# Block 2's latent attention: two heads together in the column halves of TensorE, and query tiles packed six for eight

## The chip, the core and the metric

The kernel runs on one core of one Trainium2 chip. Such a core has five engines, each with its own queue of instructions: TensorE (matrix products into the accumulator memory PSUM; called PE in the profile, and PEld for its weight loads), VectorE (DVE), ScalarE (ACT), GpSimd (POOL) and SyncE (SP, which here issues the weight transfers). The metric is the device time of one execution in microseconds (us); lower is better. All data are fp32. A dense product is made of three TensorE products of operands split into a high and a low part (line 416, `mm3`: 420, 421 and 422 are its three matmuls), in a one-pass type. A plain fp32 matmul shows in the profile as two MATMUL instructions, each of which takes a column of the moving operand in about twice the time.

## The reference

Two blocks of a model, each of two layers, on 256 tokens of width 1024; the second block has a second stream, a context of 256 tokens. What matters here is the attention in each mixing layer of the second block: eight heads, with queries and keys of 64 plain and 32 rotated features, and values of 64.

```python
def mla_q(q_lat, q_norm, w_uq, cos, sin):
    q = (rmsnorm_2(q_lat, q_norm) @ w_uq).reshape(b, n, MLA_HEADS, QK_NOPE + QK_ROPE)
    q_nope, q_rope = q[..., :QK_NOPE], q[..., QK_NOPE:]
    q_rope = apply_axial_rope(q_rope, cos, sin)
...
def attend(q_nope, q_rope, k_nope, k_rope, v):
    s = (jnp.einsum("bqhd,bkhd->bhqk", q_nope, k_nope)
         + jnp.einsum("bqhr,bkr->bhqk", q_rope, k_rope)).astype(jnp.float32) * ATTN_SCALE
    p = jax.nn.softmax(s, axis=-1).astype(v.dtype)
    return jnp.einsum("bhqk,bkhd->bqhd", p, v)
```

The latent `q_lat` has 384 features. In the first mixing layer (l = 0) the queries of the 256 tokens look at 512 keys (tokens and context), and the context's own 256 queries at the context's 256 keys. In the second (l = 1) only the tokens have queries, with 512 keys. In the diff and below, ns is the number of streams with queries, 2 and then 1.

## The kernel before

Weights come in one stream of units of at most 128 x 1024, in the order of a plan; SP loads them some units ahead, and ACT and DVE split each into its two parts (lines 393 and 394) up to three ahead of its use. The framework sets the order of instructions in each engine's queue before the run, by priority in the order of the program and by what it estimates to be ready; so a product may stand in the trace between two steps that follow each other in the code.

`mix` (line 1210) is one mixing layer. After the projections, the Fourier mixer and the convolution it makes the attention:

- Keys, K: four products, for two heads each, copied into a tile for each head of 128 rows with the rotated key rows beside the plain ones (lines 1266 to 1269).
- Queries: `queries` (line 1356) makes one 128-row tile for each head out of a weight that is padded with zeros: 3 tiles of the latent times 3 matmuls, nine for a head, over 512 columns in layer 0 and 256 in layer 1. ACT copies it out of PSUM (line 1368), and `rope2` (line 1346) rotates its 32 rows by a matmul over 256 columns (line 1349, two instructions) and three DVE operations (lines 1352 to 1354). It is a generator; `attend` calls its steps a pair of heads ahead, the first pair's lie before the values.
- Values, V: tokens on the partitions, four tiles (line 1280 copies them).
- `attend` (line 1391) goes through blocks of one head and 128 queries: in layer 0, for each of four pairs of heads, 4 blocks with 512 keys and then 4 with 256, 32 blocks in all; in layer 1, 16 blocks with 512 keys.

A block is, in this order: scores by one fp32 matmul (line 1375); softmax with queries on the partitions (`softmax_rows`: maximum on DVE, line 818; times minus the scale, 819; exponential on ACT, 479, with its sums read out behind it; reciprocal, 823, and product with it, 825, on DVE); and two blocks later (`AHEAD`) `values`: transposes of the weights on TensorE, one for 128 keys (line 1385), a copy of them by ACT into a tile `pt` (1387), and the product with the values, 128 queries by 64 features for 128 keys each (line 1389, two instructions a product, four products for 512 keys). This last one takes 64 of TensorE's 128 columns: those of the upper or the lower half, as its output rows do, by the head (a = 0 or 1). An accumulator `o` in PSUM takes a pair of heads and 256 queries, and ACT copies it out (line 1413).

PSUM has eight banks of 512 columns, handed out by name: three for `mm` (scores, dense products), three for `ax` (transposes, rotations, and `o`), one each for `nm` (sums of the norms) and `md`. Afterwards the output projection (`project_out`, key "mo") runs over all eight tiles of the mixers; its first products may start on the tiles that are there.

Of the kernel before, what the change touches and what calls it, by code (L numbers as in the profile page):

```python
# [16 lines left out]
T = 256  # L17
# [11 lines left out]

# ---------------------------------------------------------------- weight stream  # L30
# A unit is a [128, n] tile of weights, n <= 1024, made of blocks
# (array, leading index, first row, first column, width).

# [13 lines left out]
def _spread(units, mods, every):  # L47
    """The modulation units one by one between the others: the first three at once."""
    out, mods = mods[:3], mods[3:]
    for i, u in enumerate(units):  # L50
        out.append(u)
        if i % every == every - 1 and mods:
            out.append(mods.pop(0))
    return out + mods


def _evenly(units, mods, a, b, kind="acc"):
    """The modulation units evenly between the units a to b from the end."""
# [21 lines left out]
def _mix_units(l):  # L80
# [7 lines left out]
    for p in range(4):  # L88
        if p == 1:
            u.append(("mat", ("uv", l), [("w_ukv_v", l, kt * 128, 0, 512) for kt in range(2)]))  # L90
        u.append(("mat", ("uq", l, p), [("w_uqp", l, kt * 128, (2 * p + i) * 128, 128)
                                        for i in range(2) for kt in range(3)]))
# [52 lines left out]
def pack_weights(inp):  # L145
# [11 lines left out]
    qp = np.zeros((2, 384, 8, 128), np.float32)  # L157
    qp[:, :, 0::2, 0:96] = uq[:, :, 0::2]
    qp[:, :, 1::2, 0:32] = uq[:, :, 1::2, 64:]
    qp[:, :, 1::2, 64:128] = uq[:, :, 1::2, :64]  # L160
    arr["w_uqp"] = qp.reshape(2, 384, 1024)
# [11 lines left out]
# ---------------------------------------------------------------- small vectors and constants  # L173
# [48 lines left out]
def constants():  # L222
    """Masks, rotations, the DFT and the axial rotation tables: functions of the shapes alone."""
# [66 lines left out]
class Unit:  # L290
# [4 lines left out]
# Tiles of each phase: tag -> (columns, buffers)  # L295
# [16 lines left out]
class Builder:  # L312
# [26 lines left out]
    # ---- tiles  # L339
# [34 lines left out]
    # ---- weights  # L374
# [32 lines left out]
    def flush(self, n=len(PLAN)):  # L407
        """The modulation units that stand next in the stream, up to n."""
# [7 lines left out]
    def mm3(self, out, u, j, ah, al, start, stop, w=128):  # L416
        """out += W[:, block j]^T a"""
# [6 lines left out]
    def mmt(self, out, ah, al, u, j, start, stop, w=512):  # L424
        """out += a^T W[:, block j]"""
# [6 lines left out]
    def gemm(self, u, h, c0, c1, p=None):  # L432
        """One 128-feature tile of a product over the tiles of h, columns c0..c1."""
# [6 lines left out]
    def lead(self, units, h, c0, c1):  # L440
        """The same for some units at once, tile by tile of h as they come."""
# [7 lines left out]
    def pair(self, tag, n):  # L449
        """The two parts of an operand, in one tile or two."""  # L450
# [5 lines left out]
    def split(self, src, hi, lo):  # L456
        """hi + lo = src, each exact in one pass."""
# [4 lines left out]
    def table(self, name):  # L462
        """The scalar engine's table set from here on, in the order of the program."""
# [7 lines left out]
    def after(self, i, j):  # L471
        """Instruction i goes to its engine's queue behind j."""
# [3 lines left out]
    def act(self, out, src, func, **k):  # L476
        """A function of the scalar engine that needs a table."""
# [41 lines left out]
    def settle(self):  # L519
        """The sums over the partitions that are due."""  # L520
# [30 lines left out]
    def gain(self, name, l, gname, ch):  # L551
        """g * (1 + scale), per stream."""
# [56 lines left out]
    def enter(self, st, ns, A, B, lead):  # L609
        """h = x * r * A + B, split, stream by stream; lead starts on each stream as it is ready."""  # L610
# [9 lines left out]
    def enter_raw(self, st, A, B):  # L620
        """r, and for each tile of x the parts of x * A with those of B as more columns (an even number): of a product over
        them, the columns times r plus the last one are the product over x * r * A + B."""
# [27 lines left out]
    def project_out(self, units, src, ns, gate, st, tail=True):  # L650
        """x += gate * W^T src, tile by tile; the last tiles stream by stream, so that the norm of one
        stream runs beside the products of the other. With one stream, the first tiles at once, so that the
        last of src has time to arrive."""
# [16 lines left out]
    # ---- swiglu  # L670
    def ffn(self, key, st, ns, A, B, gate, more, before_last=None):
        """x += gate * swiglu(x * r * A + B); returns the sums of squares of the new x."""
# [53 lines left out]
    # ---- block 1, layer 0: softmax heads and stick-breaking heads  # L726
# [26 lines left out]
    def vproj(self, key, h):  # L753
        """Values with tokens on the partitions: two tiles [128, 512]."""
# [16 lines left out]
    def headsplit(self, src):  # L771
        """A tile of two heads' rows, each head in its own copy with zeros for the other."""
# [5 lines left out]
    def av(self, pt, v, hp):  # L778
        """Output rows of a pair of heads from their weights [k, (k0 q0, k0 q1, k1 q1)]."""
# [576 lines left out]
    def queries(self, l, p, ql, no):  # L1356
# [3 lines left out]
        for i in range(3):  # L1360
            if last is not None:
                self.rope2(last, slice(64, 96) if i == 1 else slice(0, 32))
# [229 lines left out]
```

## Time and profile before

| | |
|---|---|
| median of 3 runs | 2563.02 us (2561.24 to 2563.8) |
| span of the profiled execution, first to last instruction | 2561.5 us |
| TensorE (PE) busy in the span | 98% |
| VectorE (DVE) busy | 66% |
| ScalarE (ACT) busy | 44% |
| GpSimd (POOL) busy | 8% |
| mean granted TensorE clock | 0.996 of full |

The profile has one execution; no time of its own is given for that but its span, which lies 1.5 us under the median of the runs. Busy time on PE runs from the start of a matmul to its modelled end, so consecutive matmuls overlap and a busy PE isn't one at its peak: what a matmul costs in a stream is the distance from its start to the next start. The attention lies at 1339 to 1421 us (layer 0) and 2286 to 2337 us (layer 1) of the span.

### The profile page before, as it was taken

The numbers are of one execution on the slowest core, as the hardware profiler recorded it, in microseconds if no ns is written. First come the engines' busy times: TensorE is split into PE (matmuls) and PEld (weight loads), VectorE is DVE, ScalarE is ACT, GpSimd is POOL, SyncE is SP. The second block draws the span as 40 slices with busy tenths as digits, with TensorE's granted clock in tenths as the row PEclk, the third lists the DMA queues.
The fourth block names the chain that finished last, engine by engine and source line by source line (L and its number), as shares of the span: only waits on it lengthen the run. The fifth ranks groups of instructions, "written<-read, shape, count | busy, mean of one in ns | idle before, by whom it ended". The sixth has DMA issues, their size and how long they took to land.

```text
span 2561.5 us, 39957 instructions
## 1 busy us (share of the span) xinstructions
PE 2501.8 (98%) x15915; PEld 2177.1 (85%) x15915; DVE 1689.1 (66%) x2607; ACT 1128.5 (44%) x1955; POOL 195.9 (8%) x183
## 2 busy tenths in 40 slices
PE   6999999999999999999999999999999999999998
PEld 5878998988999887878886888888888888888998
DVE  6857768765887957774646474565656565675665
ACT  4556456565645523233525432323432323555544
POOL 1004100423000100001000100000100000101000
PEclk9999999999999999999999999999999999999999
DMA  8767656324875545663220243454244453232553
GB/s 333 268 209 244 212 188 208 116 83 158 286 248 181 189 160 188 187 197 124 79 79 26 70 154 110 146 175 144 91 159 162 150 178 122 92 109 83 190 183 97
DMA packets 117402, 408.38 MB, mean 159 GB/s; under 512 B 13024, under 2 KB 16352, under 8 KB 117216
## 3 DMA queue, kind: packets, MB, share of 16 engines
q1 hardware_dynamic: 114192, 403.08, 47.8%
q10 hardware_dynamic: 3024, 2.75, 0.4%
q8 instruction: 125, 2.05, 0.3%
q14 instruction: 61, 0.50, 0.1%
HBM read 404.74 MB, written 1.05 MB: 158 GB/s over the span
## 4 chain that ended last, share of the span: by engine, by line
PE 93%; DVE 3%; DMA 2%; ACT 1%; issue 1%; POOL 0%; ACTq 0%; DVEq 0%; SPq 0%
PE pmm L420 25%; PE pmm L422 25%; PE pmm L421 25%; PE pmd L516 2%; PE pax L1389 2%; PE pax L1072 2%; PE pmm L1375 1%; DMA r<-w 1%; PE pax L421 1%; PE pax L422 1%; PE pax L420 1%; PE pax L1385 1%; DVE l L394 1%; PE pnm L607 1%; PE pmm L429 0%
## 5 line engine op out<-in xcount | busy, mean ns | idle before, releaser
L393 ACT CAST h<-r 128x1024 fp32r<-128x1024 f32 (+3 forms) x545 | 550.2, 1016 | 1025.5 <-PE pmm L421 937.6
L394 DVE TENSOR_TENSOR l<-r,h 128x1024 fp32r<-128x1024 f32 (+3 forms) x545 | 658.6, 1213 | 306.0 <-ACT h L393 296.1
L420 PE MATMUL pmm<-h,h 128*128 128x512 f32 (+1 forms) x1928 | 674.3, 351 | 6.7 <-ACT h L640 2.3
L421 PE MATMUL pmm<-h,h 128*128 128x512 f32 (+1 forms) x1928 | 669.1, 348 | 2.0 <-DVE h L641 1.9
L422 PE MATMUL pmm<-h,l 128*128 128x512 f32 (+1 forms) x1928 | 668.9, 347 | 1.0 <-DVE l L394 1.0
L420 PEld LDWEIGHTS pmm<-h,h 128*128 128x128 f32 x1928 | 365.3, 190 | 64.4 <-issue 9.3
L421 PEld LDWEIGHTS pmm<-h,h 128*128 128x128 f32 x1928 | 365.5, 190 | 49.6 <-DVE h L641 3.2
L422 PEld LDWEIGHTS pmm<-h,l 128*128 128x128 f32 x1928 | 365.3, 190 | 47.6 <-DVE l L394 1.5
L420 PE MATMUL pmm<-hid,h 128*128 128x256 f32 (+1 forms) x1053 | 349.5, 332 | 0.0
L422 PE MATMUL pmm<-hid,l 128*128 128x256 f32 (+1 forms) x1053 | 347.5, 330 | 0.3 <-DVE l L394 0.3
L421 PE MATMUL pmm<-hid,h 128*128 128x256 f32 (+1 forms) x1053 | 347.4, 330 | 0.0
L510 DVE SCALAR_TENSOR_TENSOR macc<-r,cond,macc 128x1024 f32<-128x1024 f32 x266 | 330.0, 1281 | 0.3 <-DMA r<-w 0.2
L420 PE MATMUL pmm<-hb,h 128*128 128x258 f32 x1008 | 287.3, 285 | 7.0 <-DVE s L681 6.4
L422 PE MATMUL pmm<-hb,l 128*128 128x258 f32 x1008 | 285.8, 284 | 0.0
L421 PE MATMUL pmm<-hb,h 128*128 128x258 f32 x1008 | 285.3, 283 | 0.0
L420 PEld LDWEIGHTS pmm<-hid,h 128*128 128x128 f32 x1053 | 200.1, 190 | 20.3 <-ACT h L393 1.2
L422 PEld LDWEIGHTS pmm<-hid,l 128*128 128x128 f32 x1053 | 200.1, 190 | 18.7 <-DVE l L394 0.5
L421 PEld LDWEIGHTS pmm<-hid,h 128*128 128x128 f32 x1053 | 200.1, 190 | 18.2
L647 DVE SCALAR_TENSOR_TENSOR x<-pmm,mod_w_mod,x 128x256 f32<-128x256 f32 x188 | 84.6, 480 | 176.5 <-PE pmm L422 176.2
L420 PEld LDWEIGHTS pmm<-hb,h 128*128 128x128 f32 x1008 | 191.6, 190 | 9.8 <-DVE s L681 7.2
L422 PEld LDWEIGHTS pmm<-hb,l 128*128 128x128 f32 x1008 | 192.4, 191 | 0.4 <-issue 0.4
L421 PEld LDWEIGHTS pmm<-hb,h 128*128 128x128 f32 x1008 | 192.4, 191 | 0.3 <-DVE hb L630 0.2
(337 smaller groups left out, 2891.7 us busy)
## 6 DMA issues: line engine op xcount, KB each, us to landing
r<-w SPq DMA_DIRECT2D x665, 512.0 KB, 4.3
r<-w SPq DMA_DIRECT2D x96, 448.0 KB, 3.3
r<-w SPq DMA_DIRECT2D x16, 256.0 KB, 3.0
r<-w SPq DMA_DIRECT2D x8, 384.0 KB, 3.4
const<-const SPq DMA_DIRECT2D x2, 960.0 KB, 6.1
x<-xT ACTq DMA_DIRECT2D x8, 128.0 KB, 4.6
x<-ctxT ACTq DMA_DIRECT2D x8, 128.0 KB, 3.4
out<-x ACTq DMA_DIRECT2D x4, 128.0 KB, 2.1
```

Source lines behind the costliest of these rows:

```text
L393: nc.scalar.copy(h[:, :n], r[:, :n])
L394: nc.vector.tensor_tensor(lo[:, :n], r[:, :n], h[:, :n].bitcast(F32), op=OP.subtract)
L420: nc.tensor.matmul(out, wh, ah, start=start, stop=False)
L421: nc.tensor.matmul(out, wh, al, start=False, stop=False)
L422: nc.tensor.matmul(out, wl, ah, start=False, stop=stop)
L510: self.nc.vector.scalar_tensor_tensor(a, r, w, a, op0=OP.mult, op1=OP.add)
L516: self.nc.tensor.matmul(p[32 * g:32 * g + 32, :256], w, r[:, 256 * g:256 * g + 256], start=start, stop=stop)
L607: nc.tensor.matmul(p, self.ones, s[:, cg], start=tot == 1, stop=True)
L647: self.nc.vector.scalar_tensor_tensor(v, p[:, s * T - c0:s * T + T - c0], gate[:, 8 * s + m:8 * s + m + 1], v, op0=OP.mult, op1=OP.add)
L1072: nc.tensor.matmul(p[:, s], a[:, s], b[:, s], start=True, stop=True)
L1375: self.nc.tensor.matmul(s, q, k, start=True, stop=True)
L1389: nc.tensor.matmul(o, V[b], pt[:, 128 * b:128 * b + 128], start=b == 0, stop=b == nb - 1)
```

## The change

The attention goes through blocks of two heads. A block's scores and softmaxes are made for both heads; two blocks later both are transposed and copied (`turned`, which now stands ahead of the next block's scores in the program, while the product with the values stands behind them), and their products with the values are issued in turns, a product of the one head and one of the other. `o` moves from the three `ax` banks to the one `nm` bank. The query weight is packed without zeros: two tiles with the 32 rotated rows of four heads each, which are rotated whole, and four tiles with the 64 plain rows of two heads each. A head's tile is put together from both: ACT copies the plain half, DVE the rotated rows, and POOL sets 32 rows of the odd heads to zero. Even heads have 96 rows in queries and keys. There is one more `tmp` tile, and the plan has three units for the queries in place of four. Lines that are only blank or comments are left out, and so are the old bodies, which stand above.

```diff
-    for p in range(4):
-        if p == 1:
+    u.append(("mat", ("ur", l), [("w_uqr", l, kt * 128, r * 128, 128) for r in range(2) for kt in range(3)]))
+    for i in range(2):
+        u.append(("mat", ("un", l, i), [("w_uqn", l, kt * 128, (2 * i + j) * 128, 128)
+                                        for j in range(2) for kt in range(3)]))
+        if i == 0:
             u.append(("mat", ("uv", l), [("w_ukv_v", l, kt * 128, 0, 512) for kt in range(2)]))
-        u.append(("mat", ("uq", l, p), [("w_uqp", l, kt * 128, (2 * p + i) * 128, 128)
-                                        for i in range(2) for kt in range(3)]))
...
-    arr["w_uqp"] = qp.reshape(2, 384, 1024)
+    arr["w_uqn"] = uq[:, :, :, :64].reshape(2, 384, 512)
+    arr["w_uqr"] = uq[:, :, :, 64:].reshape(2, 384, 256)
...
-    "mix": {"h": (512, 18), "t": (256, 2), "raw": (512, 6), "tmp": (512, 4), "o": (512, 8), "pt": (512, 4), "ru": (256, 1)},
+    "mix": {"h": (512, 18), "t": (256, 2), "raw": (512, 6), "tmp": (512, 5), "o": (512, 8), "pt": (512, 4), "ru": (256, 1)},
...
-        self.rope2(kr, slice(0, 128))
+        self.rope2(kr)
...
-        queries = [self.queries(l, p, ql, no) for p in range(4)]
         u = self.get(("uk", l))
...
-                K += [a, b]
-        Q = list(queries[0])
+                K += [a[0:96], b]
+        qr = self.rotated(l, ql, no)
+        first = self.queries(l, 0, ql, qr, no)
         u = self.get(("uv", l))
...
-        self.attend(Q, queries, K, V, ns, out)
+        self.attend(lambda p: self.queries(l, p, ql, qr, no) if p else first, K, V, ns, out)
...
+        nc.vector.tensor_tensor(u, ps[:, :T], tab[:, T:], op=OP.mult)
+        nc.vector.tensor_tensor(t[:, :T], t[:, :T], tab[:, :T], op=OP.mult)
+        nc.vector.tensor_tensor(t[:, :T], t[:, :T], u, op=OP.add)
+
+    def latent(self, u, j, ql, no):
+        ps = self.mm()
+        for kt in range(3):
+            self.mm3(ps[:, :no], u, 3 * j + kt, ql[kt][0], ql[kt][1], kt == 0, kt == 2)
+        return ps[:, :no]
+
+    def rotated(self, l, ql, no):
+        u = self.get(("ur", l))
+        out = []
+        for r in range(2):
+            q = self.t("raw")
+            self.nc.scalar.copy(q[:, :no], self.latent(u, r, ql, no))
+            out.append(q)
+        for q in out:
+            self.rope2(q)
+        return out
+
+    def queries(self, l, p, ql, qr, no):
+        nc = self.nc
+        if p % 2 == 0:
+            self.un = self.get(("un", l, p // 2))
+        ps = self.latent(self.un, p % 2, ql, no)
+        a, b = self.t("raw"), self.t("raw")
+        r, j = qr[p // 2], 64 * (p % 2)
+        nc.gpsimd.memset(b[32:64, :no], 0.0)
+        nc.vector.tensor_copy(a[64:96, :no], r[j:j + 32, :no])
+        nc.vector.tensor_copy(b[0:32, :no], r[j + 32:j + 64, :no])
+        nc.scalar.copy(a[0:64, :no], ps[0:64])
+        nc.scalar.copy(b[64:128, :no], ps[64:128])
+        return a[0:96], b
...
+    def turned(self, P):
+        n = P.shape[-1]
+        p = self.ax()[:, :n]
+        for b in range(n // 128):
+            self.nc.tensor.transpose(p[:, 128 * b:128 * b + 128], P[:, 128 * b:128 * b + 128], self.ident)
+        pt = self.t("pt")[:, :n]
+        self.nc.scalar.copy(pt, p)
+        return pt
+
+    def attend(self, queries, K, V, ns, out):
+        nc = self.nc
+        Q = {0: queries(0)}
+        blocks = [(p, s, qt) for p in range(4) for s in range(ns) for qt in range(2)]
+        P, o = {}, None
         for i in range(len(blocks) + AHEAD):
+            pts = [self.turned(w) for w in P.pop(i - AHEAD)] if i >= AHEAD else None
             if i < len(blocks):
+                p, s, qt = blocks[i]
                 q0, k0 = s * T + 128 * qt, s * T
+                P[i] = [self.weights(Q[p][a][:, q0:q0 + 128], K[2 * p + a][:, k0:]) for a in range(2)]
+                if i % (2 * ns) == 2 * ns - 2 and p < 3:
+                    Q[p + 1] = queries(p + 1)
+            if pts:
+                p, s, qt = blocks[i - AHEAD]
+                if qt == 0:
+                    o = self.psum("nm", 1)
+                nb = 4 - 2 * s
+                for b in range(nb):
+                    for a in range(2):
+                        h = slice(128 * p + 64 * a, 128 * p + 64 * a + 64)
+                        nc.tensor.matmul(o[64 * a:64 * a + 64, 128 * qt:128 * qt + 128], V[2 * s + b][:, h],
+                                         pts[a][:, 128 * b:128 * b + 128], start=b == 0, stop=b == nb - 1)
+                if qt == 1:
+                    nc.scalar.copy(out[p][:, s * T:s * T + T], o[:, :T])
```

## Rows read from the trace of the kernel before

**Rows 1.** The profile's first part: busy us, share of the span, instructions of each engine.

```profile
PE 2501.8 (98%) x15915; PEld 2177.1 (85%) x15915; DVE 1689.1 (66%) x2607; ACT 1128.5 (44%) x1955; POOL 195.9 (8%) x183
```

**Rows 2.** The chain of work that ended last, shares of the span by engine.

```profile
PE 93%; DVE 3%; DMA 2%; ACT 1%; issue 1%; POOL 0%; ACTq 0%; DVEq 0%; SPq 0%
```

**Rows 3.** Busy time by stretch (start:end, length; busy us and instructions; clock).

```profile
1339.00:1421.00 82.00, 81.10 (x433) 54.02 (x432) 51.85 (x158) 47.85 (x122) 0.00 (x0) 1.00 0.08 27
2286.00:2304.00 18.00, 16.82 (x93) 11.39 (x92) 15.10 (x38) 10.95 (x25) 0.00 (x0) 1.00 0.17 58
...
2286.00:2337.00 51.00, 49.82 (x300) 34.81 (x300) 34.32 (x94) 29.35 (x70) 0.00 (x0) 1.00 0.13 42
```

**Rows 4.** Groups of instructions, 1339 to 1421 us: count, busy us, mean ns, idle before.

```profile
L1389 PE MATMUL pax<-pt,h 128*64 128x128 f32 x192 | 27.5, 281 | 0.9 <-ACT pt L1387 0.6
...
L825 DVE TENSOR_SCALAR tmp<-tmp,s 128x512 f32<-128x512 f32 x16 | 7.7, 484 | 0.2
L479 ACT ACTIVATE tmp<-pmm,s 128x256 f32<-128x256 f32 x16 | 7.6, 480 | 0.6 <-DVE s L819 0.6
L818 DVE TENSOR_REDUCE s<-pmm 128x1 f32<-128x256 f32 x16 | 6.6, 415 | 1.1 <-PE pmm L1375 1.0
...
L825 DVE TENSOR_SCALAR tmp<-tmp,s 128x256 f32<-128x256 f32 x16 | 5.6, 351 | 0.1
...
L1349 PE MATMUL pax<-raw,const 128*128 128x256 f32 x12 | 3.9, 405 | 0.0
...
L1353 DVE TENSOR_TENSOR raw<-raw,const 32x256 f32<-32x256 f32 x6 | 2.4, 405 | 0.0
```

**Rows 5.** The same for 2286 to 2337 us.

```profile
L1389 PE MATMUL pax<-pt,h 128*64 128x128 f32 x128 | 16.8, 279 | 0.0
```

**Rows 6.** Timeline at two places where two value products follow each other (start, length).

```profile
1409.10 1.89 PE L1389 MATMUL pax<-pt,h 128*64 128x128 f32 x16
...
1409.26 0.58 ACT L1387 COPY pt<-pax 128x512 f32<-128x512 f32 x1 [0.28 <-PE pax L1385]
...
1410.92 0.48 PE L1375 MATMUL pmm<-h,raw 128*128 128x256 f32 x1
...
2332.51 1.58 PE L1389 MATMUL pax<-pt,h 128*64 128x128 f32 x16
```

**Rows 7.** Timeline: one modulation product in four column quarters.

```profile
78.34 0.64 PE L516 MATMUL pmd<-macc,pick 128*32 128x256 f32 x8
```

**Rows 8.** Timeline: dense matmuls over 512 and 256 columns, and a rotation.

```profile
1330.98 0.39 PE L422 MATMUL pmm<-h,l 128*128 128x512 f32 x1
1331.21 0.39 PE L420 MATMUL pmm<-h,h 128*128 128x512 f32 x1
1331.44 0.63 PE L1349 MATMUL pax<-raw,const 128*128 128x256 f32 x2
...
2285.46 0.28 PE L422 MATMUL pmm<-h,l 128*128 128x256 f32 x1
2285.58 0.28 PE L420 MATMUL pmm<-h,h 128*128 128x256 f32 x1
```

**Rows 9.** Waits, first two of 1339 to 1421 us, then two of 2286 to 2337 us.

```profile
PEld pax L1389 <- ACT pt L1387: 13.1, 27, 0.8
DVE s L823 <- ACT tmp L479: 13.1, 17, 1.4
...
PEld pax L1389 <- ACT pt L1387: 2.8, 6, 0.8
PEld pax L1389 <- ACT o L1413: 0.8, 1, 0.8
```

**Rows 10.** Timeline of one head's softmax in layer 1.

```profile
2330.10 0.69 DVE L818 TENSOR_REDUCE s<-pmm 128x1 f32<-128x512 f32 x1 [2.47 <-PE pmm L1375]
...
2331.07 0.69 ACT L479 ACTIVATE tmp<-pmm,s 128x512 f32<-128x512 f32 x1 [0.69 <-DVE s L819]
...
2332.08 0.48 DVE L825 TENSOR_SCALAR tmp<-tmp,s 128x512 f32<-128x512 f32 x1
```

More of the change, by code (lines that the diff above doesn't have):

```diff
@@ L156, in pack_weights @@
     uq = inp["w_uq_2"].reshape(2, 384, 8, 96)
[L157 to L160, printed above, removed]
-    arr["w_uqp"] = qp.reshape(2, 384, 1024)
+    arr["w_uqn"] = uq[:, :, :, :64].reshape(2, 384, 512)
+    arr["w_uqr"] = uq[:, :, :, 64:].reshape(2, 384, 256)
     out = np.empty(WTOTAL, np.float32)
@@ L1344, in conv, with rope2 @@
         return out
-    def rope2(self, t, rows):
+    def rope2(self, t):
         nc = self.nc
@@ L1351, in rope2 @@
         tab = self.c["rope2"]
-        nc.vector.tensor_tensor(u[rows], ps[rows, :T], tab[rows, T:], op=OP.mult)
-        nc.vector.tensor_tensor(t[rows, :T], t[rows, :T], tab[rows, :T], op=OP.mult)
-        nc.vector.tensor_tensor(t[rows, :T], t[rows, :T], u[rows], op=OP.add)
-    def queries(self, l, p, ql, no):
-        u = self.get(("uq", l, p))
-        last = None
-        for i in range(3):
-            if last is not None:
-                self.rope2(last, slice(64, 96) if i == 1 else slice(0, 32))
-            if i < 2:
-                ps = self.mm()
-                for kt in range(3):
-                    self.mm3(ps[:, :no], u, 3 * i + kt, ql[kt][0], ql[kt][1], kt == 0, kt == 2)
-                q = self.t("raw")
-                self.nc.scalar.copy(q[:, :no], ps[:, :no])
-            yield last
-            last = q
+        nc.vector.tensor_tensor(u, ps[:, :T], tab[:, T:], op=OP.mult)
[29 more added lines that the diff above has]
+        return a[0:96], b
     def weights(self, q, k):
@@ L1378, in weights @@
         return P
-    def values(self, P, V, o):
-        nc = self.nc
-        nb = len(V)
-        p = self.ax()[:, :128 * nb]
-        for b in range(nb):
-            nc.tensor.transpose(p[:, 128 * b:128 * b + 128], P[:, 128 * b:128 * b + 128], self.ident)
-        pt = self.t("pt")[:, :128 * nb]
-        nc.scalar.copy(pt, p)
-        for b in range(nb):
-            nc.tensor.matmul(o, V[b], pt[:, 128 * b:128 * b + 128], start=b == 0, stop=b == nb - 1)
-    def attend(self, Q, queries, K, V, ns, out):
-        Q = {0: Q}
-        blocks = [(p, s, a, qt) for p in range(4) for s in range(ns) for a in range(2) for qt in range(2)]
-        per, P, o = 4 * ns, {}, None
+    def turned(self, P):
[6 more added lines that the diff above has]
+        return pt
@@ L1397, in attend @@
+    def attend(self, queries, K, V, ns, out):
+        nc = self.nc
+        Q = {0: queries(0)}
+        blocks = [(p, s, qt) for p in range(4) for s in range(ns) for qt in range(2)]
+        P, o = {}, None
         for i in range(len(blocks) + AHEAD):
+            pts = [self.turned(w) for w in P.pop(i - AHEAD)] if i >= AHEAD else None
             if i < len(blocks):
-                p, s, a, qt = blocks[i]
-                j = i % per - per // 2
-                if p < 3 and -3 < j < 1:
-                    Q.setdefault(p + 1, []).append(next(queries[p + 1]))
+                p, s, qt = blocks[i]
@@ L1403, in attend @@
                 q0, k0 = s * T + 128 * qt, s * T
-                P[i] = self.weights(Q[p][1 + a][:, q0:q0 + 128], K[2 * p + a][:, k0:])
-            if i >= AHEAD:
-                p, s, a, qt = blocks[i - AHEAD]
-                if a == qt == 0:
-                    o = self.ax()
-                h = slice(128 * p + 64 * a, 128 * p + 64 * a + 64)
-                self.values(P.pop(i - AHEAD), [v[:, h] for v in V[2 * s:]],
-                            o[64 * a:64 * a + 64, 128 * qt:128 * qt + 128])
-                if a == qt == 1:
-                    self.nc.scalar.copy(out[p][:, s * T:s * T + T], o[:, :T])
+                P[i] = [self.weights(Q[p][a][:, q0:q0 + 128], K[2 * p + a][:, k0:]) for a in range(2)]
```

## The prediction

> **What bounds the kernel now.** I read the busy shares first: PE 98% of the span, DVE 66%, ACT 44% [rows 1]. A busy PE need not be a full one, so next the chain that ended last: 93% of it is PE [rows 2]. Work taken from PE's queue is therefore worth its stream time, unless the stage it leaves has another limit. The two stages that change come next [rows 3]: in layer 0 PE is busy 81.10 of 82 us, with DVE at 51.85 and ACT at 47.85; in layer 1 it is 49.82 of 51, with 34.32 and 29.35, and all of the idle 1.18 us lie in the first 18 us, where DVE is busy 15.10. The clock is 1.00 throughout. So PE bounds both stages, with DVE and ACT at six tenths. The groups, timelines and waits then give the price of each part.
>
> **Values, two heads in turns.** The value products are 192 instructions in layer 0 and 128 in layer 1 [rows 4, 5]. Sixteen in a row take 1.89 us at 281 ns each: (1.89 - 0.28) / 15 = 0.107 us from start to start [rows 4, 6]. The stream is 320 x 0.107 = 34.2 us. Do the halves run side by side? That place is two heads' products in a row and it went one by one, but the second head's `pt` copy ran there from 1409.26 to 1409.84 [rows 6], when the first head's eight (0.86 us from 1409.10) were nearly through. At 2332.51, where `pt` was there earlier, sixteen took 1.58 us [rows 6]: the tail of one head's products overlapped the head of the other's. The stronger row is the modulation product: eight instructions in four column quarters take 0.64 us [rows 7]; one by one, at the 0.22 us of a 256-column fp32 instruction (0.63 - 0.405, rows 4 and 8 being the same form), they would take over 1.7. So quarters overlap fully, and I take the halves at full overlap: half of 34.2, **17.1 us** less. The bounds are 0 (no overlap) and 17.1.
>
> The Trainium skill, "TensorE: Matmul & The Clock Gate", Part 3 (measured speedup against the span model), gives 2.38x for three column tiles, less than three. Scaled to two tiles (1.59x) that would be an estimate of 12.7 us, and the forecast 4.4 us later; the eight instructions above, with no such loss for four tiles, speak against it, and I don't take it.
>
> **Query tiles, six for eight.** Nine matmuls fewer for each of two tiles, 18 a layer. Dense matmuls start 0.23 us apart over 512 columns and 0.12 over 256 [rows 8]: 18 x 0.23 + 18 x 0.12 = **6.3 us**. Three tiles now lie ahead of the scores where two did, so the stages lose 27 matmuls each and the stretch before them gains nine.
>
> **Rotations.** Two whole tiles in place of eight heads: six rotations, 12 instructions, fewer a layer; 24 x 0.22 us = **5.3 us** of PE. DVE loses 18 operations of 0.405 us a layer, 7.3 us [rows 4], and gains copies of 32 rows; none is in the trace, and their bounds are the 256-wide operation at 0.35 and the 512-wide at 0.48, SBUF to SBUF [rows 4]. I take these for layer 1 and layer 0: six within the stage, 2.9 and 2.1 us. ACT makes two half-height copies a pair instead of two whole ones, no change in count, and two more before the scores; these, the rotations and the first copies hide behind the first plain tile and the values' products, over 24 dense matmuls of 0.23 (5.5 us) that don't need them. Without that cover the chain would cost six operations of 0.405 and a copy of 0.48, 2.9 us a layer. POOL's zeros cost nothing: POOL is idle in both stages [rows 3]; on the path each would cost about the 0.48 of the wide DVE operation. Scores over 96 rows in place of 128 stream the same columns, no gain. One weight unit fewer a layer, and its DMA and split, lie off PE.
>
> **Turning from one form to another.** At 1409.10 the sixteenth product starts at 1410.71, and the next score at 1410.92 [rows 6]: 0.21 us where 0.107 would do, so 0.1 is lost on leaving the 64-column form. Entering isn't shown by itself; between 0 and the same. Groups of value products fall from 48 (one a block) to 24: 2.4 to 4.8 us, taken as **4**.
>
> Sum off PE's queue: 17.1 + 6.3 + 5.3 + 4 = **32.7 us**.
>
> **What is late next.** Without new waits layer 0's stage would last 82 - 10.3 - 6.2 - 2.6 - 2.7 = 60.2 us, and layer 1's 51 - 6.8 - 3.2 - 2.6 - 1.3 = 37.1. DVE in them: 51.85 - 7.3 + 2.9 = 47.5 and 34.32 - 7.3 + 2.1 = 29.1, ACT 47.85 and 29.35: all about 0.8 of the stage, against six tenths before. The one stretch of before where DVE stands so high (15.10 of 18, 0.84) lost 1.18 / 18 = 6.6% of PE [rows 3]. I charge that to both stages: 0.066 x 97.3 = **6.4 us**. Bounds: 0 below, and the softmax rival's price above. What speaks for less is the new order: PE waited 13.1 and 2.8 us for `pt` before value products [rows 9], and now a block's two scores stand between the transposes and the products.
>
> `o` in one bank adds a wait: the first value product of a pair and stream needs ACT's copy of the `o` before. Behind it in PE's queue stand the next block's transposes and scores, for which DVE and ACT then wait. Two transposes and two scores lie between the last product of the one and the first of the next, so I take nothing; the longest such wait before was 0.8 us [rows 9], and 12 of these would be 9.6.
>
> Gain 32.7 - 6.4 = 26.3; span 2561.5 - 26.3 = 2535.2. The median of the runs was 1.5 above the span: **2537 us**.
>
> **Rivals.**
> 1. *The new order also removes waits.* If half of the 15.9 us of `pt` waits goes and the 6.4 is not paid, the gain is 32.7 to 40.7: 2522 to 2530. For it: the order above. Against it: PE idled for only 0.9 of the 82 us [rows 3], so other products already fill most of these waits, and with the queries there are fewer of those.
> 2. *Softmax becomes the limit.* A 512-key head takes from 2330.10 to 2332.56, 2.46 us from maximum to weights [rows 10]; a 256-key head is shorter by (0.69 - 0.415) + (0.69 - 0.48) + (0.484 - 0.351) = 0.62 [rows 4, 10], so 1.84. If DVE and ACT took heads strictly in turn, that would be 16 x 4.30 = 68.8 us in layer 0 and 39.4 in layer 1, 10.9 over the 97.3: gain 21.8. DVE's other work is at most 47.5 - 16 x (0.69 + 0.415 + 0.484 + 0.351) = 16.5 us in layer 0 and 29.1 - 16 x (0.69 + 0.484) = 10.3 in layer 1, part of it small steps that the 2.46 already holds; if half came in series too, the gain would be 8.4. That is 2541 to 2555, and I put it at 2549. For it: DVE waited 13.1 us for ACT's sums in layer 0 [rows 9]. Against: chains of two heads do overlap there now, and a block offers two at once. The Trainium skill, "TensorEngine Tiling (Array Packing)", Performance Considerations, says the same as a rule: tiling speeds up TensorE but not the emptying of PSUM, which may become the bottleneck. The trace of before can't show it, since no engine but PE is near its limit there.
> 3. *The halves don't overlap.* Gain 32.7 - 17.1 - 6.4 = 9.2: 2554. Against it stand the overlaps above.
> 4. *Slower: the single bank of `o`.* If each of the 12 hand-overs stalled PE, at 0.8 us the time would be 2546; it decides from (26.3 + 5) / 12 = 2.6 us each, when ACT's copy stands behind two exponentials and two `pt` copies each time: 2568 and more. The rows show a third of that at most.
>
> **How the numbers follow.** Within 0.2% (5 us, 2558 to 2568) a measurement can't tell a change from none. Chances: forecast with its loss of some 0 to 12 us (2530 to 2543) 0.50; rival 1 0.17; rival 2 0.19; rival 3 0.04; rival 4, wholly or with the others, 0.10, half of it within 0.2% and half beyond. So faster 0.90, same 0.05, slower 0.05. The range runs from 2524 to 2555: it takes in rivals 2 and 3 and most of rival 1, and leaves out about 0.15.
>
> **What would show it.** Value products in the timeline: 16 instructions in about 1.1 us (8 x 0.107 + 0.28) where 1.89 stood; if 1.9, rival 3. Dense matmuls with the queries' operand down by 18 and rotation instructions from 18 to 6 a layer. Stages of about 64 and 39 us; if they stay over 70 and 44, with PE idle and its waits ending in `tmp` or `pt`, rival 2; waits of value products for `o`'s copy over 1 us, rival 4. What would make it wrong without any of these: another order of the queues that leaves PE idle before the scores, or a change in stages that the edit doesn't touch.

## The result, and the profile after

The changed kernel takes 2532.04 us, the median of 4 runs (2531.09 to 2532.76), where the kernel before took 2562.9 beside it: a ratio of 0.9879 with a 95% interval of 0.9866 to 0.9893. That is 30.9 us; the forecast was 26.3 less, 2537 in a range of 2524 to 2555. The span of the profiled execution went from 2561.5 to 2529.8 us.

The profile's first part and the chain that ended last, after the change, as in [rows 1, 2]:

```profile
PE 2472.3 (98%) x15855; PEld 2155.0 (85%) x15855; DVE 1679.2 (66%) x2585; ACT 1127.6 (45%) x1957; POOL 199.8 (8%) x191
...
PE 92%; DVE 3%; ACT 1%; DMA 1%; issue 1%; POOL 1%; DVEq 0%; ACTq 0%; POOLq 0%
```

The shares say nothing of 31 us; PE still bounds the kernel. From the first score to the end of the last value product, layer 0's stage went from 81.2 to 59.6 us and layer 1's from 50.1 to 37.6: 34.1 less. The three stretches outside them gave back 2.4 (1.0 ahead of layer 0, 0.9 between the stages, 0.6 behind). Busy time by stretch, as in [rows 3], and then the first 6 us of each stage:

```profile
1340.00:1400.00 60.00, 58.74 (x387) 37.87 (x386) 44.65 (x142) 45.76 (x120) 0.52 (x1) 1.00 0.08 28
2266.00:2305.00 39.00, 38.45 (x268) 25.18 (x267) 29.75 (x80) 28.83 (x69) 0.30 (x1) 1.00 0.12 42
...
1340.00:1346.00 6.00, 4.74 (x17) 2.34 (x16) 5.43 (x13) 3.25 (x7) 0.00 (x0) 1.00 0.26 90
2266.00:2272.00 6.00, 5.45 (x24) 3.23 (x23) 5.78 (x15) 4.99 (x12) 0.00 (x0) 1.00 0.01 3
```

DVE and ACT rose from six tenths to about three quarters, not to the 0.8 of the forecast, and PE idles for 1.26 and 0.55 us. (Busy time runs to the modelled ends, so these rows don't hold the short gaps counted below.) All of it lies in the first 6 us of each stage, with DVE nearly full: the first softmaxes, before any product with the values is ready. In layer 0 it is one wait of a score, put down to ACT's exponential, which reads the bank that the score will take:

```profile
1344.01 1.56 PE L1392 MATMUL pmm<-h,raw 128*128 128x512 f32 x4 [1.26 <-ACT tmp L477]
```

The timeline of PE in layer 0, against [rows 6] (start, length):

```profile
1352.80 1.02 PE L1392 MATMUL pmm<-h,raw 96*128 96x512 f32 x2
1353.76 1.09 PE L1431 MATMUL pnm<-pt,h 128*64 128x128 f32 x16
1354.78 0.44 PE L1402 MATMUL pax<-const,tmp 128*128 128x128 f32 x2
...
1357.20 1.88 PE L1392 MATMUL pmm<-h,raw 96*128 96x512 f32 x4
1359.02 0.66 PE L1431 MATMUL pnm<-pt,h 128*64 128x128 f32 x8
```

Sixteen value products take 1.09 us where 1.89 stood, and eight take 0.66: the two halves run side by side. (Counts of value products are instructions here, two for each product.) The rows also price the turn that the forecast could see only on one side. Four scores of 512 columns start 0.427 us apart, so those from 1357.20 are through with their columns at 1358.91; the first value product starts at 1359.02, 0.1 later. The sixteen end theirs at 1354.68, and the next transpose starts at 1354.78, again 0.1 later. From start to start, entering costs 0.098 us and leaving 0.096 on the mean of the 37 groups of value products in both stages; there were 46 before.

The waits of layer 0's stage, as in [rows 9], and one of layer 1's:

```profile
PEld pnm L1431 <- ACT pt L1404: 3.2, 7, 0.8
PEld pmm L1392 <- ACT tmp L477: 3.1, 4, 2.1
PEld pnm L1431 <- ACT tmp L477: 3.1, 6, 0.8
...
DVE s L821 <- ACT tmp L477: 1.9, 7, 0.4
...
PEld pnm L1431 <- ACT o L1434: 0.8, 1, 0.8
...
PEld pnm L1431 <- ACT pt L1404: 3.0, 4, 0.8
```

In layer 0 the waits put down to `pt` fell from 13.1 to 3.2 us, in layer 1 they did not (2.8 and 3.0); those of DVE for ACT's sums fell from 13.1 to 1.9. The rows of PEld are not idle time of PE: the queue of weight loads stands still while PE is busy with the scores ahead. The same 0.76 us stands before the value products at 1370.33, whose last `pt` copy had ended at 1369.20, and is put down to ACT's exponential, which they don't read. By PE's starts, entering the value products cost 1.5 us beyond the turns before the change (both stages) and 0.1 after. Scores' weight loads wait 3.1 us for an `mm` bank that ACT's exponential still reads; 1.26 of it idles PE, as shown above. Put down to `o`'s single bank is one wait of 0.8. Rotations (line 1347) are 12 instructions in the whole program:

```profile
L1347 PE MATMUL pax<-raw,const x12: 377/379/484, 1272.0 to 2260.8; 128*128 128x256 f32 x12
```

**Where the time came from.** For each PE instruction in the stages I took the distance to the next start that it has in an undisturbed stream (scores 0.427 and 0.213 us, transposes and value products 0.107, rotations 0.213, dense 0.227 and 0.115), laid these times side by side, and counted what they cover together; the rest is gaps. A turn is counted at 0.192 us, in and out. Scores and transposes are the same on both sides. Both stages, us:

| | before | after | change | forecast |
|---|---|---|---|---|
| dense matmuls, in the stages | 21.2 | 11.4 | -9.8 | |
| the stretches outside | | | +2.4 | |
| query tiles, both together | | | -7.4 | -6.3 |
| rotations | 5.1 | 0 | -5.1 | -5.3 |
| dense matmuls that start early behind another form | -2.2 | -0.4 | +1.7 | |
| value products, less what runs side by side | 33.8 | 20.1 | -13.7 | -17.1 |
| turns (46 and 37 groups) | 8.8 | 7.1 | -1.7 | -4.0 |
| other gaps: waits, first fills | 13.3 | 7.8 | -5.5 | +6.4 |
| sum | | | -31.7 | -26.3 |

The fifth row is a correction: behind a transpose, a rotation or a score, some dense matmuls start sooner than that form takes in its stream, and there were more such places before (2.2 us, and 0.4 after). The value products themselves overlapped by 0.5 us of 34.2 before, and by 14.1 after. That is not all of 17.1, because in 11 of the 24 blocks the framework put the first head's first product ahead by itself. Its counterpart then runs alone too:

```profile
1346.81 0.43 PE L1431 MATMUL pnm<-pt,h 128*64 128x128 f32 x2
...
1347.43 0.88 PE L1431 MATMUL pnm<-pt,h 128*64 128x128 f32 x12
```

At 1364.20 the fourteen that are left take 1.09 us, as long as sixteen in turns. The 2.4 us outside are put down to the nine dense matmuls a layer that moved ahead of the scores (3.1 by their spacing). That isn't shown: experiment 3 has the same nine, and there the stretch between the stages grew by 0.2 us, not 0.9. A few matmul records can be missing, and they would count as gaps.

### The profile page after: what moved, and what is told of

The parts are those of the page before. It is cut to its first block, busy times and chain, and to the rows that moved or that the text cites. A ratio compares the mean times of both kernels' runs of the same rounds, so it can differ in the third digit from the quotient of the medians.

```text
span 2529.8 us, 39830 instructions
## 1 busy us (share of the span) xinstructions
PE 2472.3 (98%) x15855; PEld 2155.0 (85%) x15855; DVE 1679.2 (66%) x2585; ACT 1127.6 (45%) x1957; POOL 199.8 (8%) x191
## 4 chain that ended last, share of the span: by engine, by line
PE 92%; DVE 3%; ACT 1%; DMA 1%; issue 1%; POOL 1%; DVEq 0%; ACTq 0%; POOLq 0%
PE pmm L418 26%; PE pmm L420 25%; PE pmm L419 25%; PE pmd L514 2%; PE pax L1070 2%; PE pmm L1392 1%; PE pax L420 1%; PE pax L419 1%; PE pax L418 1%; DMA r<-w 1%; PE pnm L1431 1%; PE pax L1402 1%; DVE l L392 1%; PE pnm L605 1%; PE pmm L427 0%
## 5 line engine op out<-in xcount | busy, mean ns | idle before, releaser
L391 ACT CAST h<-r 128x1024 fp32r<-128x1024 f32 (+2 forms) x543 | 548.7, 1016 | 1022.0 <-PE pmm L419 947.3
L392 DVE TENSOR_TENSOR l<-r,h 128x1024 fp32r<-128x1024 f32 (+2 forms) x543 | 656.4, 1214 | 307.8 <-ACT h L391 298.5
```

Of the source, the lines that this page charges most:

```text
L391: nc.scalar.copy(h[:, :n], r[:, :n])
L392: nc.vector.tensor_tensor(lo[:, :n], r[:, :n], h[:, :n].bitcast(F32), op=OP.subtract)
```

## The experiments

All are timed against the kernel before, in five rounds; the stages are measured as above, in the profiled execution. The changed kernel's line is the first.

| | median us | ratio, 95% interval | stages us |
|---|---|---|---|
| changed kernel | 2532.0 | 0.9879, 0.9866 to 0.9893 | 59.6, 37.6 |
| 1 head by head | 2537.8 | 0.9898, 0.9882 to 0.9913 | 61.6, 39.7 |
| 2 new attention alone | 2549.8 | 0.9945, 0.9933 to 0.9958 | 70.8, 45.4 |
| 3 query tiles alone | 2549.0 | 0.9942, 0.993 to 0.9955 | 70.5, 44.4 |
| 4 transposes behind | 2537.6 | 0.99, 0.9886 to 0.9913 | 61.2, 40.0 |
| 5 `o` among the ax banks | 2533.7 | 0.9885, 0.987 to 0.99 | 59.8, 38.2 |
| 6 one DVE copy more | 2534.1 | 0.9886, 0.9873 to 0.99 | 61.4, 38.8 |
| 7 one column half | 2545.7 | 0.9933, 0.992 to 0.9945 | 66.5, 42.6 |
| 8 values of two blocks | 2529.3 | 0.9868, 0.9855 to 0.9882 | 57.4, 35.5 |
| 9 four mm banks | 2527.9 | 0.9858, 0.9841 to 0.9874 | 57.7, 36.4 |
| 10 as 8, in order | 2528.3 | 0.9863, 0.9848 to 0.9878 | 56.8, 35.8 |
| 11 two DVE copies more | 2539.5 | 0.9905, 0.9891 to 0.992 | 65.1, 38.7 |
| 12 as 10, four mm banks | 2527.1 | 0.986, 0.9844 to 0.9877 | 56.0, 37.2 |

**1. Head by head.**

```diff
-                for b in range(nb):
-                    for a in range(2):
+                for a in range(2):
+                    for b in range(nb):
```

> The changed kernel, but in each block all products with the values of the first head, then all of the second; the same instructions in the same column halves. Theory A (the two halves run side by side, and that is worth the largest term): the products go one by one again at 0.107 us, except where the tail of the one head meets the start of the other, which saved 0.31 us in 16 before the change. So 320 x 0.107 / 2 = 17.1 us come back less up to 24 x 0.31 = 7.4: 2542 to 2549 us, and 16 products take 1.6 to 1.9 us. Rival O (the gain comes from the order of the work, the overlap lies in time in which TensorE would have waited): less than 5 us come back, 2532 to 2537.

5.8 us came back by the medians, near rival O's 5 and under theory A's 10 to 17. But the edit doesn't take the overlap away: 7.9 of the 14.1 us stay, as its timeline shows:

```profile
1355.91 1.58 PE L1431 MATMUL pnm<-pt,h 128*64 128x128 f32 x16
...
1358.65 0.67 PE L1431 MATMUL pnm<-pt,h 128*64 128x128 f32 x8
```

Of the sixteen, the second head's first product started at 1356.40, when the first head had started five of its eight (from 1355.91), and the two ran side by side from there. Its `pt` had been there since 1356.18, and 11 of the groups of sixteen overlap by the same 0.36 us, so it isn't a late operand that sets this. Of eight products, four a head, the second head's started 0.01 us behind the first's, so these overlap wholly in either order. The expectation was wrong, since products of the other half start past a few that still wait. The trace doesn't record the order within the queue, so that PE does this, and not the framework's order, is inferred. To take the overlap away, both heads must share a half.

**7. Both heads in one column half.** The products stand head by head, and ACT copies each head out by itself.

```diff
-                        nc.tensor.matmul(o[64 * a:64 * a + 64, 128 * qt:128 * qt + 128], V[2 * s + b][:, h],
+                        nc.tensor.matmul(o[0:64, T * a + 128 * qt:T * a + 128 * qt + 128], V[2 * s + b][:, h],
...
-                    nc.scalar.copy(out[p][:, s * T:s * T + T], o[:, :T])
+                    for a in range(2):
+                        nc.scalar.copy(out[p][64 * a:64 * a + 64, s * T:s * T + T], o[0:64, T * a:T * a + T])
```

> The changed kernel with the values of both heads of a block in the same 64 columns of TensorE: the second head's sums go to other columns of the same rows of the bank, head by head, and ACT copies each head's 64 rows out by itself, 12 more copies. Nothing of one head's products can then run beside the other's. Theory A (the starts within both stages show 14.5 us of value products that run beside others after the change): 2532 + 14.5 = 2546.5 us, 2544 to 2549. The forecast's term of 17.1: 2549 and above. Rival O (the overlap lies in time in which TensorE waits anyway): 2538 to 2541, as little more than the order head by head cost.

```profile
1353.93 1.96 PE L1431 MATMUL pnm<-pt,h 128*64 128x128 f32 x16
...
1358.22 1.09 PE L1431 MATMUL pnm<-pt,h 128*64 128x128 f32 x8
```

Sixteen products take 1.96 us and eight 1.09: one by one. No overlap is left, and 13.7 us came back by the medians. (The 14.5 of the expectation holds 0.4 of dense matmuls; the value products' own overlap is 14.1.) The stages grew by 11.8: the 14.1, less 1.7 for turns, as there are 28 groups in place of 37, and less 0.9 for six dense matmuls that lie outside them here; the other gaps grew by 0.6, and early starts took 0.3. The overlap is worth about its stream time, and rival O falls.

**2 and 3. Each part alone.** The second is the kernel before with `attend` and `turned` of the changed one, five `tmp` tiles, and the old `queries`; the third is the changed kernel with the old `values` and `attend` and four `tmp` tiles. The line that joins them:

```diff
-                    Q[p + 1] = queries(p + 1)
+                    Q[p + 1] = list(queries[p + 1])[1:]
...
-                    Q.setdefault(p + 1, []).append(next(queries[p + 1]))
+                    Q[p + 1] = queries(p + 1)
```

> The kernel before with the new attention alone: two heads to a block, their products in turns, transposes ahead of the scores, the accumulator in its own bank; the query tiles are the eight padded ones with their eight rotations. Theory A (the terms add up): the 6.3 us of matmuls and 5.3 us of rotations of the packing are missing, so 2532.0 + 11.6 = 2543.6 us, 2541 to 2546. Rival W (vector work limits the new attention: with the 7.3 us of rotations a layer back on DVE, the new order waits more): 2548 to 2555. Rival O (all from the order and the overlap, the packing hidden): 2532 to 2536.

> The changed kernel's query tiles, six for eight with two rotations a layer, and the kernel before's attention: one head to a block, transposes behind the scores directly ahead of the values, the accumulator among the ax banks. Theory A (the terms add up): 2562.9 - 11.6 = 2551 us, 2549 to 2554. Rival F (the dense products that go were the filler that hid the 13.1 us of waits for pt; without them TensorE idles): 2555 to 2563.

By the ratios the parts give 0.0055 and 0.0058, 14.1 and 14.9 us; together 29.0, where both at once give 31.0. The intervals are some 3 us to each side, so they add up as far as can be told. The query tiles alone gave no less than theory A's 11.6 us, so rival F (lost cover for the waits) is refuted. The new attention alone came out in rival W's range. By the starts its overlap is nearly that of the changed kernel (13.7 us, 14.1 there), but the gaps with the turns fell by 2.3 us only, and by 2.2 in experiment 3, where both parts together took 7.2 off them. Whether the rotations on DVE hold it up, as rival W has it, or the dense products in PE's queue, isn't settled. DVE's share speaks against W in layer 0: 0.72 in experiment 2, no more than the 0.74 of the changed kernel; in layer 1 it is 0.80 against 0.76.

```profile
1339.90:1410.80 70.90, 69.57 (x425) 45.47 (x424) 51.17 (x158) 46.38 (x121) 0.00 (x0) 1.00 0.10 31
2276.90:2322.40 45.50, 43.65 (x298) 29.38 (x298) 36.20 (x94) 29.12 (x69) 0.00 (x0) 1.00 0.15 47
```

**4. Transposes behind the scores again.**

```diff
-            pts = [self.turned(w) for w in P.pop(i - AHEAD)] if i >= AHEAD else None
...
-            if pts:
+            if i >= AHEAD:
+                pts = [self.turned(w) for w in P.pop(i - AHEAD)]
```

> The changed kernel with the transposes of a block behind the next block's scores, directly ahead of its products with the values, as before the change. Theory A (what the forecast rests on: the order matters little, since other products fill the waits for pt): 2532 to 2536 us. Rival O (the new order removed the 15.9 us of waits for pt, and these come back, half or all): 2540 to 2548 us, with waits of value products for pt of 8 us or more in the first stage.

5.5 us by the medians, 4.0 of them in the two stages: gaps 2.4, overlap 1.4 (12.8 us in place of 14.1), turns 0.8, and dense matmuls 0.5 less. Layer 0's waits are longer:

```profile
PEld pnm L1431 <- ACT pt L1404: 5.2, 10, 0.8
DVE s L821 <- ACT tmp L477: 5.1, 9, 0.9
```

Both were lower in the changed kernel (3.2 and 1.9). PE itself lost 0.2 us beyond the turns on entering the value products, so it isn't `pt` that it waited for; the gaps between scores grew from 2.1 to 3.9 us. The order is worth some 4 to 5.5 us: between the two theories, and a smaller share of the gain than the overlap. Even with the old order, `pt` waits stay far under the 13.1 of [rows 9].

**5. `o` back among the ax banks.**

```diff
-                    o = self.psum("nm", 1)
+                    o = self.ax()
```

> The changed kernel with the accumulator o back among the three ax banks, which the transposes use too; the nm bank stays empty in the attention. Theory A (the single bank costs nothing, as the forecast says, and the transposes of two heads want the three ax banks): 2532 to 2536 us. Rival B (the hand-over of the single bank stalls the products with the values): 2526 to 2530 us.

2533.7: no gain, and no difference that can be told. The single bank costs nothing that these runs can tell; the slower rival of the forecast has no ground.

**6 and 11. One and two more DVE operations a head.**

```diff
         self.softmax_rows(s[:, None, :], 1, ATTN_SCALE, P[:, None, :])
+        self.nc.vector.tensor_copy(P[:, :256], P[:, :256])
```

> The changed kernel with one more DVE operation a head, a copy of 256 columns of the weights onto themselves behind the product with the reciprocal, some 0.28 us by the 32-row copies of that width in the changed kernel; 48 of them, 13.4 us, which takes DVE from three quarters to nine tenths of both stages. Theory A (TensorE bounds the stages and the vector work has slack): 2532 to 2535 us. Forecast's charge (6.6% of the stages are lost when DVE stands at 0.84 or more): 2538 to 2540. Rival 2 (the chain of the softmaxes sets the stages, each operation comes in series): 2543 to 2546.

> The changed kernel with two more DVE copies a head in place of one; one took DVE from 44.65 to 51.8 us in the first stage and cost 2.0 us in all. Two take it to 58.9 of 59.6 us and 38.6 of 37.6, so that DVE has as much work as TensorE. Theory A (slack until an engine is full): the second copy begins to bind, 2535 to 2540 us. Rival 2 (the chain of the softmaxes sets the stage, every copy comes in series): 2 x 13.4 = 27 us more, 2555 to 2560; the forecast's charge, 6.6% of the stages and more: 2538 to 2545.

Busy time by stage, first with one copy (0.287 us each), then with two:

```profile
1341.00:1402.40 61.40, 59.78 (x388) 38.06 (x386) 51.26 (x174) 46.05 (x119) 0.52 (x1) 1.00 0.09 27
2268.90:2307.70 38.80, 37.64 (x261) 24.28 (x259) 32.11 (x95) 28.27 (x67) 0.44 (x1) 1.00 0.13 42
```

```profile
1343.30:1408.40 65.10, 61.80 (x393) 39.20 (x392) 56.05 (x206) 46.34 (x120) 0.52 (x1) 1.00 0.08 26
2273.70:2312.50 38.80, 37.56 (x262) 24.13 (x262) 33.69 (x111) 28.95 (x68) 0.64 (x1) 1.00 0.13 42
```

With one, DVE stands at 0.83 of both stages, where the forecast charged 6.6%; the stages grew by 1.8 and 1.1 us, 3% of them, and the time by 2.0, which is within the noise. With two the time grew by 7.5. The copies add less than their 0.287 us each: by the starts one takes 0.20 us (from 1360.22 to 1360.42 in experiment 6), since it begins before the one ahead has ended. DVE's busy time in the stages rose by 9.0 us with one and by 15.3 with two, so the expectations' 13.4 and 27 were too high. Still, the stages have slack for about half of what was added, and rival 2, by which all of it would come in series, is refuted for them as a whole. Of layer 0's 5.5 us with two copies, 1.6 are seven dense matmuls that fell into the stage there.

**8 and 10. Fewer turns.** Experiment 8 issues the products of both query tiles of a pair together. Experiment 10 also queues every transpose, score and value product behind the one before it.

```diff
+                held.append(pts)
                 if qt == 1:
+                    o = self.psum("nm", 1)
+                    nb = 4 - 2 * s
+                    for q in range(2):
+                        for b in range(nb):
+                            for a in range(2):
...
+    def chain(self, i):
+        if self.last_pe is not None:
+            self.after(i, self.last_pe)
+        self.last_pe = i
```

> The changed kernel with the products with the values of two blocks (both query tiles of a pair of heads) issued together, once for each pair and stream: 12 groups in place of 24. Theory T (entering and leaving the 64-column form costs 0.096 us each time): 12 x 0.19 = 2.3 us less, 2529 to 2530. Rival L (the weights' tiles are held longer, so their copies and the next transposes wait): 2532 to 2538.

> The kernel with the values of two blocks together, and with TensorE's queue held in the attention to the order of the program: each transpose, score and product with the values is queued behind the one before it (dense products may still stand between them). Theory T (each entering and leaving of the 64-column form costs 0.096 us; the groups are now really 12, where 27 stood in the run before and 37 in the changed kernel): 15 x 0.19 = 2.9 us less than the run before, 2526 to 2527. Rival L (the free order filled waits, and without it TensorE waits for weights that the softmaxes and copies have not brought yet): 2530 to 2540.

Experiment 8 gave 2.7 us where theory T asked for 2.3, but not in its way alone: the framework's order left 27 groups, not 12, and the turns fell from 7.1 to 5.2 us. In experiment 10 there are 12, the turns cost 2.3 us, 0.19 a group, and 16.1 us of the values overlap (14.8 in experiment 8); but the stages fell by 0.3 us only. The other gaps took the rest back, from 7.8 to 11.5: the first stage's scores now wait 4.4 us for a bank (3.1 in the changed kernel), and transposes for DVE.

```profile
PEld pmm L1392 <- ACT tmp L477: 4.4, 4, 2.1
...
PEld pax L1407 <- DVE tmp L823: 1.1, 2, 0.9
```

**9 and 12. Four mm banks and two ax banks,** in the changed kernel and in experiment 10's.

```diff
-        return self.psum("mm", 3)
+        return self.psum("mm", 4)
...
-        return self.psum("ax", 3)
+        return self.psum("ax", 2)
```

> The changed kernel with four PSUM banks for mm and two for ax in place of three and three, in the whole program. In the changed kernel scores wait for a bank of mm behind ACT's exponentials (gaps between scores of 1.7 and 0.4 us in the two stages). Theory M (these waits go): 2530 to 2531 us. Rival X (two ax banks make the transposes of two heads wait for their copies, and the sums, rotations and first products elsewhere wait too): 2534 to 2545.

> The kernel with the values of two blocks together in the order of the program, and four mm banks with two ax banks. Theory A (two separate gaps of TensorE, the turns from form to form and the scores that wait for a bank): both gains add up, 4 us by the turns and 3 us by the banks against the changed kernel, the stages together some 89 to 91 us where the changed kernel has 97.2, and 2524 to 2526 us. Rival X (in a fixed order two ax banks make transposes wait, and those hold the scores up): stages of 93 us and more, 2528 to 2532.

Experiment 9 saves 4 us, 3.2 of them in the stages; layer 0's waits of scores for a bank fell from 3.1 to 1.7:

```profile
PEld pmm L1392 <- ACT tmp L477: 1.7, 2, 1.2
```

PE's wait at the start of that stage fell from 1.26 to 0.40. But the banks are the smaller part of the 3.2: PE's gaps between scores fell by 0.7 us, while fewer groups (30 for 37) gave 1.3 and more overlap about 1.

In experiment 12 the two gains did not add up: 2527.1 us, within the uncertainty of 9 and 10, with stages of 93.2 us. Layer 1's stage is 1.4 us longer than in experiment 10, and lost it at its start. The timeline of PE and DVE there, and busy time by stretch:

```profile
2268.32 0.66 PE L1407 MATMUL pax<-const,tmp 128*128 128x128 f32 x4 [2.19 <-DVE tmp L823]
2268.82 3.33 PE L1392 MATMUL pmm<-h,raw 96*128 96x512 f32 x4
...
2266.66 1.22 DVE L392 TENSOR_TENSOR l<-r,h 128x1024 fp32r<-128x1024 f32 x1
2267.79 0.48 DVE L823 TENSOR_SCALAR tmp<-tmp,s 128x512 f32<-128x512 f32 x1
```

```profile
2264.00:2266.00 2.00, 2.00 (x8) 0.89 (x7) 1.96 (x7) 2.00 (x6) 0.18 (x1) 1.00 0.00 0
2266.00:2268.00 2.00, 0.14 (x2) 0.00 (x0) 1.94 (x6) 1.93 (x6) 0.13 (x1) 1.00 0.00 0
2268.00:2270.00 2.00, 1.68 (x6) 1.03 (x7) 2.00 (x7) 1.14 (x3) 0.00 (x0) 0.78 0.35 68
2270.00:2272.00 2.00, 2.00 (x4) 0.73 (x3) 1.97 (x5) 0.29 (x2) 0.00 (x0) 0.50 0.50 203
2272.00:2274.00 2.00, 2.00 (x17) 2.00 (x16) 0.84 (x2) 0.45 (x2) 0.00 (x0) 0.87 0.68 254
```

A transpose, fixed in its place, waited 2.19 us for DVE, which had a weight's split of 1.22 us ahead of the softmax's last product, and no score behind it could pass. The four scores behind it took 3.33 us, at the lower clock of the last rows, where four take 1.88 in the changed kernel.

## Why the prediction was right, and where its steps were not

- **Time and direction.** Right: the stages lost 34.1 us, 26.9 of them stream on PE and 1.7 turns, and PE still bounds them. The forecast's stages without new waits, 60.2 and 37.1 us, are nearly those measured (59.6 and 37.6); by its parts that is luck, as follows.
- **Query tiles and rotations.** Right: 10.8 us by the starts (7.4, if the 2.4 us outside belong to it, and 5.1, less 1.7 for the early starts), for 11.6; experiment 3 gives both together, 14.9, with 11.5 to 17.9 by its interval.
- **Values in two halves: the mechanism was right, the size was not.** 13.7 us, not 17.1. The step "I take the halves at full overlap" holds within a group that is issued whole (16 in 1.09 us), but not for the stage: after the change 14.1 of the 17.1 overlap, since in 11 of the 24 blocks the framework's order splits the group. And 0.5 us of the stream ran side by side before, most of it at the place in [rows 6] (16 in 1.58 us), which the forecast used for the overlap without taking it off the stream. Experiment 7 prices the overlap at 13.7 by the medians. The Trainium skill, "TensorE: Matmul & The Clock Gate", Part 3, would have given an estimate of 12.7, nearer than mine, but by luck: the trace shows no loss of that kind in a group that is issued whole.
- **Turning.** The price was right (0.096 to 0.098 us each way, now seen on both sides), the count was not: "48 to 24" was 46 to 37, since the framework's order puts transposes and scores between the products of a block.
- **New waits: wrong in sign.** "I charge that to both stages" took 1.18 us of idle in the first 18 us of layer 1 for a rate that goes with DVE's share. It is a cost of the start: after the change all idle time of PE lies in the first 6 us of each stage. Nor was that "the one stretch of before where DVE stands so high": in layer 0, from 1339 to 1345 us, DVE was busy for 5.02 of 6 us and PE for all 6. At the same DVE share over a whole stage, experiment 6 measured 3%, not 6.6%, and DVE stood at three quarters, not 0.8. In place of a loss of 6.4 the other gaps fell by 5.5, spread over many small ones; 1.4 of it is on entering the value products, and no run separates the rest.
- **Rival 1 was half true.** The new order removes waits, and the 6.4 wasn't paid; experiment 4 puts the order at 4 to 5.5 us, against up to 8 in the rival. But the 15.9 us of `pt` waits that the rival halves were mostly no idle time of PE, which lost 1.5 us there. With 3.4 us too much for the values, 2.3 for the turns and 0.8 for queries and rotations, the 11.9 of the waits leave the forecast 5.4 us off the span: errors of two signs that nearly met.
- **Rivals 2 to 4.** Rival 2 doesn't hold for the stages (experiments 6 and 11), rival 3 falls by experiment 7, rival 4 by experiment 5. What the Trainium skill says of emptying PSUM ("TensorEngine Tiling (Array Packing)", Performance Considerations), that tiling doesn't speed it up and it may become the limit, shows in a small way: the weight loads of layer 0's scores wait 3.1 us for banks that ACT hasn't read out (1.0 before), and PE idles for 1.26 of it.

Open remain the 2 us by which both parts together seem to beat their sum (within the intervals), what made up most of the 5.5 us of other gaps, and a stretch ahead of the attention that was up to 3 us longer in some profiled executions: layer 0 begins at 1340.0 us in the changed kernel, and at 1343.2 and 1343.3 in experiments 9 and 11.

## What to carry to other kernels

Before halving a stream, ask in how many places both halves will stand in the queue together: here the groups that were issued whole overlapped fully, but for one, and 11 of 24 blocks were split. Lay the starts of the trace next to each other; a wait of the weight-load queue isn't idle time of PE. A loss seen at the start of a stage is paid once, not as a rate; look where in the stage the idle time lies before scaling it. When a bound engine's work shrinks, look next at banks and order: one more bank for scores, and products grouped by form, took 3 to 5 us more (2527 to 2529 us, ratio 0.986 to 0.987), near the limit of what these runs can tell. A fixed order gave its gain back in waits.

## What the runs showed of the hardware that was not expected

- A product in the other column half starts past products that still wait in the first half: head by head, eight products of two heads took 0.67 us, as little as in turns (0.66), and of sixteen the second head's began while three of the first's were still to start. (That it is PE that passes them is inferred; see experiment 1.)
- PE's clock fell after it idled: in experiment 12 it was busy for 0.14 of 2 us, and the granted clock in the 2 us stretches behind was 0.78, then 0.50 (the level of 1.2 GHz), then 0.87. So a wait of 2.19 us cost more than itself: the four scores behind it took 1.45 us longer than in the changed kernel. In the changed kernel's stages the clock stayed at 1.00.
